# Strassen's scheme for the first layer's MLP, with the context's tokens as plain products on the same weight blocks

## The chip, the core and the metric

The kernel runs on one core of a Trainium2 chip. The metric is the device time of one execution in microseconds; the median over several executions is compared. Five engines work side by side, each through a list of instructions of its own: PE (TensorE, matrix products), DVE (VectorE), ACT (ScalarE), POOL (GpSimd) and SP (SyncE), which here only issues transfers. An instruction waits at the head of its engine's list until what it needs is there.

## What is computed

A network of two layers on 1024 latent tokens (`x`) and 256 context tokens (`ctx`), all in float32, with a model width of 1024. Layer 0 mixes tokens by attention, layer 1 by a state-space scan with a gated product behind it (GLU). After each mixer comes an MLP with a squared ReLU and 4096 hidden columns. Every norm is scaled and shifted, every residual gated, by vectors computed from conditioning weights `w_ada`. The context needs no MLP in layer 1.

```
def _mlp(h, w1, w2):
    return jnp.square(jax.nn.relu(h @ w1)) @ w2
...
    for i in range(DEPTH):
        need_ctx = i < DEPTH - 1
        m = act_lat @ w_ada[i] + b_ada[i]
        mc = act_ctx @ w_ada[i] + b_ada[i]
...
        x = x + g1 * y
        h2 = _rmsnorm(x, norm2_g[i], NORM_EPS) * (1.0 + sc2) + sh2
        x = x + g2 * _mlp(h2, mlp_w1[i], mlp_w2[i])
        if need_ctx:
            ctx = ctx + g1c * yc
            h2c = _rmsnorm(ctx, norm2_g[i], NORM_EPS) * (1.0 + sc2c) + sh2c
            ctx = ctx + g2c * _mlp(h2c, mlp_w1[i], mlp_w2[i])
    return _rmsnorm(x, final_g, NORM_EPS)
```

## The kernel before

Activations lie transposed: features on the 128 partitions, tokens along the free axis. The tokens are three blocks `BLK` (line 24): latent 0 and 1 of 512 each and the context, block 2, of 256. A float32 product is made of three fp32r matmuls, `hi*hi + hi*lo + lo*hi` (`mm3`, L328), so each operand is split first: ACT rounds the high part, DVE subtracts to get the low one (L324 and L325 for weight pages, L471 and L472 for tokens).

The stages in order are in_proj and attention, `out_proj` (L1118, matmuls into `op_acc`), the first layer's `mlp` (L1142, `m_acc`), the state-space stage (`ssm`, its first matmul is `s_X`, L1706), GLU, and the second layer's MLP `mlp_s` (L1187, `st_b`).

`out_proj` goes over the context's block first, then blocks 0 and 1. Column tile by column tile it adds the gated product to the residual streams `xl` and `xc` (L1109), which `load_x` fetches just before. `follow` with `rstd_steps` squares each finished column (L367), sums it over the partitions (L352) and so makes each token's norm factor: a power on POOL (L441), a Newton step on DVE (L447 to L449), and for a whole block a broadcast over the partitions in PSUM (`n_bc`, L398). `scaled` (L451) then multiplies the columns by it on DVE (`n_t`, L463, a ring of four tiles) and scales and shifts them on POOL (L465); `to_H` splits the result into `Hh` and `Hl`. Blocks 2 and 0 are done while `out_proj` goes on with the next block, block 1 while `mlp` has begun.

`mlp` goes over 16 slices `f` of 256 hidden columns: two weight pages for the first product, two for the second, three token blocks, 3 x 8 matmuls for each hidden tile and 3 x 2 for each output tile. Between its parts it calls `work`, a generator that does two things for later stages: 48 pages of conditioning weights of layer 1 (`ada`, L262: each page is a 512 KB load on SP's queue and eight small matmuls, L285), and 32 tables of powers for the state-space stage on POOL (`ssm_table`, L1556; its complex products are L1382 to L1387). With the last slice `last()` sets up `u_norm` (L1576), which makes the state-space stage's norm factors (`rU`, L1607) as columns are finished, copies the columns to DRAM (`xS`), and loads the gains `gU`.

`mlp_s` does the latent tokens of layer 1 by Strassen's scheme. There are four quarters of the hidden columns, and for each two units, one per weight matrix. In a unit, weights and tokens are 2 x 2 blocks, and seven products take the place of eight; each product is four k-tiles of 12 matmuls with 512 columns, so 8 x 336 = 2688 matmuls. Blocks of weights lie in a ring of five buffers `A`. Sums of weight blocks are made without an engine's arithmetic: `s1` is a load and a DMA on POOL's queue that adds a second block to it (`acc`, L1234); `s2` is `s1` negated by ACT (`neg`, L1239) with another block added; `s3` and `s4` likewise. ACT and DVE split each block (`st_a`, L1292 and L1295) and each token tile (`st_b`, L1304 and L1307); sums of token blocks are DVE's (L1219). The order on every engine is set by a planner, class `Plan` (L115): each step has an engine, a cost, a rank (due time) and steps that it needs, and the planner writes the engines' lists from these.

```
    ORDER = (1, 2, 6, 5, 7, 3, 4)
    AFTER = {6: 1, 7: 6, 4: 7, 5: 2, 3: 5}
```

## Time and profile before

| | |
|---|---|
| median of 3 runs | 3076.78 us (3076.42 to 3079.14) |
| profiled execution | 3081.73 us, span 3080.0 us |
| PE busy | 2878.7 us, 93% of the span |
| DVE, ACT, POOL busy | 1920.8, 1185.0, 1160.0 us |
| out_proj | 941.0 to 1060.5 us from the span's start |
| first layer's MLP | 1060.5 to 2003 us |
| ssm, then GLU | 2003 to 2222, to 2411 us |
| second layer's MLP | 2411 to 3080 us |

Times in the profile count from the start of the span. A group of instructions is listed with its source line, engine, operation, output and inputs, shape and count; behind the bar stand its busy time, the mean duration of one in ns, and how long its engine was idle just before such an instruction, with what ended the wait. Matmuls are pipelined: the duration of one overlaps the next, so the pace is read from start times. PEclk is the clock that TensorE was granted, 1.00 being 2.4 GHz.

### The profile page before, as it was taken

How to read it: one execution, taken by the hardware profiler on the slowest of the kernel's cores; microseconds unless marked ns; L12 is line 12 of the kernel's file. 1: busy time of each engine (PE TensorE's matmuls, PEld its weight loads, DVE VectorE, ACT ScalarE, POOL GpSimd, SP SyncE). 2: the span in 40 equal slices, each digit the busy share in tenths (PEclk: the TensorE clock that was granted, in tenths of full speed). 3: DMA queues.
4: the chain of work that ended last, by engine and by line, in shares of the span. 5: the costliest groups of instructions: out<-in, count | busy, mean ns of one | idle time of the engine just before them, and what ended most of it. 6: DMA issues, size and time to landing. Idle time of an engine off the chain costs nothing. (4 is left out here: it accounts for less than half of the span.)

```text
span 3080.0 us, 46255 instructions
## 1 busy us (share of the span) xinstructions
PE 2878.7 (93%) x17352; PEld 2377.3 (77%) x17352; DVE 1920.8 (62%) x3337; ACT 1185.0 (38%) x2211; POOL 1160.0 (38%) x2346
## 2 busy tenths in 40 slices
PE   7999998888999999999999999967699799999997
PEld 4878887777878777787888888856588688888885
DVE  3887686988664555554554545489923566666665
ACT  3322214676663321111112121245422365656563
POOL 3343233555442277777787000167623200000001
PEclk9999999999999999999999999988899899999998
DMA  6356664233543124333311111366432444554441
GB/s 241 110 187 220 206 221 143 70 90 104 154 118 140 55 97 128 108 120 101 76 60 48 44 41 42 101 184 182 125 108 75 111 117 126 125 126 125 125 110 55
DMA packets 172305, 363.47 MB, mean 118 GB/s; under 512 B 34689, under 2 KB 97185, under 8 KB 162865
## 3 DMA queue, kind: packets, MB, share of 16 engines
q1 hardware_dynamic: 162384, 310.62, 31.5%
q0 software_dynamic: 9696, 49.90, 7.5%
q8 instruction: 136, 2.23, 0.3%
q14 instruction: 89, 0.72, 0.1%
HBM read 294.97 MB, written 65.49 MB: 117 GB/s over the span
## 5 line engine op out<-in xcount | busy, mean ns | idle before, releaser
L1316 PE MATMUL st_b<-st_b,st_a 128*128 128x512 f32 x2688 | 614.2, 391 | 10.3 <-DVE st_b L1307 7.2
L1316 PEld LDWEIGHTS st_b<-st_b,st_a 128*128 128x128 f32 x2688 | 506.7, 189 | 117.8 <-DVE st_b L1307 7.8
L324 ACT ACTIVATE w_hi<-w_raw 128x1024 fp32r<-128x1024 f32 x132 | 136.7, 1053 | 460.6 <-PE m_acc L334 351.7
L333 PE MATMUL m_acc<-hid_h,w_hi 128*128 128x512 f32 (+1 forms) x768 | 277.1, 361 | 0.0
L333 PE MATMUL m_acc<-Hh,w_hi 128*128 128x512 f32 (+1 forms) x768 | 273.9, 357 | 0.0
L334 PE MATMUL m_acc<-hid_l,w_hi 128*128 128x512 f32 (+1 forms) x768 | 272.6, 355 | 0.0
L335 PE MATMUL m_acc<-Hh,w_lo 128*128 128x512 f32 (+1 forms) x768 | 272.3, 354 | 0.0
L335 PE MATMUL m_acc<-hid_h,w_lo 128*128 128x512 f32 (+1 forms) x768 | 272.1, 354 | 0.0
L334 PE MATMUL m_acc<-Hl,w_hi 128*128 128x512 f32 (+1 forms) x768 | 272.1, 354 | 0.0
L325 DVE TENSOR_TENSOR w_lo<-w_raw,w_hi 128x1024 fp32r<-128x1024 f32 x132 | 169.3, 1294 | 155.7 <-ACT w_hi L324 148.2
L1109 DVE SCALAR_TENSOR_TENSOR xl<-m_acc,m,xl 128x512 f32<-128x512 f32 x256 | 189.5, 747 | 116.4 <-PE m_acc L335 116.1
L1160 DVE TENSOR_TENSOR m_r<-m_r 128x512 f32<-128x512 f32 (+1 forms) x96 | 60.8, 635 | 229.0 <-ACT hid_h L1159 228.8
L333 PEld LDWEIGHTS m_acc<-hid_h,w_hi 128*128 128x128 f32 x768 | 145.0, 189 | 36.0 <-issue 14.4
L333 PEld LDWEIGHTS m_acc<-Hh,w_hi 128*128 128x128 f32 x768 | 145.7, 190 | 24.4 <-issue 4.5
L334 PEld LDWEIGHTS m_acc<-hid_l,w_hi 128*128 128x128 f32 x768 | 145.1, 189 | 22.9 <-issue 3.4
L335 PEld LDWEIGHTS m_acc<-Hh,w_lo 128*128 128x128 f32 x768 | 145.7, 190 | 20.3
L335 PEld LDWEIGHTS m_acc<-hid_h,w_lo 128*128 128x128 f32 x768 | 145.1, 189 | 20.6
L334 PEld LDWEIGHTS m_acc<-Hl,w_hi 128*128 128x128 f32 x768 | 145.7, 190 | 19.2
L1158 ACT ACTIVATE m_r<-m_acc 128x512 f32<-128x512 f32 (+1 forms) x96 | 50.1, 524 | 254.9 <-PE m_acc L335 254.0
L333 PE MATMUL ip_acc<-Hh,w_hi 128*128 128x512 f32 (+1 forms) x384 | 143.1, 374 | 4.1 <-ACT Hh L471 4.1
L334 PE MATMUL ip_acc<-Hl,w_hi 128*128 128x512 f32 (+1 forms) x384 | 139.3, 363 | 1.5 <-DVE Hl L472 1.2
L335 PE MATMUL ip_acc<-Hh,w_lo 128*128 128x512 f32 (+1 forms) x384 | 138.6, 362 | 0.0
(399 smaller groups left out, 6753.7 us busy)
## 6 DMA issues: line engine op xcount, KB each, us to landing
ada_raw<-in_wada_dram SPq DMA_DIRECT2D x96, 512.0 KB, 4.2
w_raw<-in_w_dram SPq DMA_DIRECT2D x64, 512.0 KB, 4.2
s_par<-pD SPq DMA_DIRECT2D x32, 864.0 KB, 4.5
at_q<-qD SPq DMA_DIRECT2D x152, 128.0 KB, 2.7
w_raw<-in_win_dram SPq DMA_DIRECT2D x24, 512.0 KB, 4.6
pD<-tb_cs POOLq DMA_DIRECT2D x32, 320.0 KB, 2.5
pD<-sl_w SPq DMA_DIRECT2D x16, 576.0 KB, 3.4
st_wa<-in_w1b_dram SPq DMA_DIRECT2D x9, 1024.0 KB, 6.3
```

The source lines that it names most:

```text
L324: nc.scalar.activation(hi[:, j], r, AF.Copy)
L325: nc.vector.tensor_tensor(lo[:, j], r, hi[:, j].bitcast(F32), ALU.subtract)
L333: nc.tensor.matmul(out, lh, rh, start=first and i == 0, stop=False)
L334: nc.tensor.matmul(out, lh, rl, start=False, stop=False)
L335: nc.tensor.matmul(out, ll, rh, start=False, stop=last and i == n - 1)
L1109: nc.vector.scalar_tensor_tensor(xv, av, gate, xv, op0=ALU.mult, op1=ALU.add)
L1158: nc.scalar.activation(r[:, :n], acc[:, :n], AF.Relu)
L1160: nc.vector.tensor_tensor(r[:, :n], r[:, :n], r[:, :n], ALU.mult)
L1316: PE.matmul(bk[p][:, mt], x, y, start=(p in (1, 2, 5) and t == 0 and i == 0), stop=(t == 3 and i == 2), skip_group_check=True)
```

## The change

Layer 0's MLP is now done by `mlp_s` too, called by `mlp0` for layer 0 and by `mlp1` for layer 1; `mlp` is gone. Each of layer 0's eight units has, beside its seven products, two plain ones for the context, `c1` ahead of them and `c2` behind them (`ctx_product`): eight k-tiles of 12 matmuls with 256 columns, on the blocks `w11`, `w12` and `w22`, `w21`. Per unit that makes 336 matmuls of 512 columns and 192 of 256. `w21` is one load more in a unit, and layer 0 has four buffers in ring `A`; layer 1 has six.

What `mlp` interleaved goes elsewhere. The 48 pages of conditioning weights move into `out_proj`, three steps of the generator after each column tile, with a ring of four pages. The gains `gU` are loaded there as well. The tables become 256 planner steps on POOL inside layer 0's `mlp_s` (`extra`). The norm factors of `out_proj`'s blocks are kept, and `norms()` scales all 24 columns behind `out_proj`, into float32 tiles `hr` that lie where `Hh` and `Hl` lay. In the last unit the squares for `u_norm` are planner steps after product 4 (both latent blocks) and after `c2` (context). In `mlp_s` of layer 0 the token sums share fewer tiles and are made again in each first unit; layer 1 keeps one of its three.

```diff
+    a["w1b"] = g["mlp_w1"].reshape(2, 2, 4, P, 4, 2, 512).transpose(0, 4, 5, 1, 3, 2, 6).reshape(2, 4, 2, 2, P, 2048)
+    a["w2b"] = g["mlp_w2"].reshape(2, 4, 2, 4, P, 2, 512).transpose(0, 1, 5, 2, 4, 3, 6).reshape(2, 4, 2, 2, P, 2048)
...
-    def out_proj(self, ps, sp):
+    def out_proj(self, ps, sp, prep):
...
         def then(b, bc):
-            self.scaled(lambda ct: self.xv0(ct, b), BLK[b][1], 0, 1, int(b == 2), bc, sp, self.to_H(b))
+            if b == 2:
+                rs[b] = sp.tile([P, BLK[b][1]], F32, name="n_bcc")
+                nc.scalar.activation(rs[b], bc, AF.Copy)
+            else:
+                rs[b] = bc
...
                     step(b, ct)
+                    prep()
...
         step()
-    def mlp(self, i, first, xv, ps, mp, prep, last):
...
+        def norms():
+            for b in (2, 0, 1):
+                scaled(b, rs[b], to=lambda ct: self.Hr[b][:, ct])
+        return norms
...
+        products = ("c1", *self.ORDER, "c2") if ctx else self.ORDER
+        for j, fn in enumerate(extra):
+            plan.add("G", 1.9, 4.0 + 2.9 * j, fn)
...
+                at[p] = now
+                now += 8 * 1.45 if p in ("c1", "c2") else 4 * PK
...
+            s1 = (u + ctx) % 2
+            X = {1: f"X{s1}", 2: f"X{1 - s1}", "c1": f"X{1 - s1}", "c2": f"X{1 - s1}"}
+            bk = {p: bank[s1 if p in (1, 6, 7, 4) else 1 - s1] for p in products}
...
+            if ctx:
+                ld["w21"] = D(at[1] + 40, F(load, "w21", (1, 0)), take=["A"])
...
+                if u == 7 and p in tail:
+                    x = [y for q in products[:products.index(p) + (p != lasts)] for t in range(4) for y in [made.get(("x", q, t))] if y]
+                    own = max(len(tail[p]) - 4, 0)
+                    for j, fn in enumerate(tail[p]):
+                        tailpe = plan.add("S", 0.6, e + 4 + 0.6 * j, fn, [*x, made["x", p, j - own] if p == lasts and j >= own else None, tailpe])
...
+    def ctx_product(self, p, u, plan, at, ld, hm, made, free, X, bk, A, T, sa, sb, hr, chid, xv, prev):
+        V, S, PE = self.nc.vector, self.nc.scalar, self.nc.tensor
+        second, m, n = u % 2, int(p == "c2"), NCTX
+        for j in range(8):
+            k = j if m == 0 else (j + 4) % 8
+            t, key, r = k % 4, f"w{m + 1}{k // 4 + 1}", at[p] + 1.45 * j
+            if t % 2 == 0:
+                sl = {}
+                def ahi(t=t, sl=sl, key=key):
+                    sl["a"] = T("a", sa)
+                    sl["w"] = A[key][:, t:t + 2]
+                    S.activation(sl["a"][:, 0], sl["w"], AF.Copy)
+                def alo(sl=sl):
+                    V.tensor_tensor(sl["a"][:, 1], sl["w"], sl["a"][:, 0].bitcast(F32), ALU.subtract)
+                ah = plan.add("S", 1.06, r - 9, ahi, [ld[key]], take=["a"])
+                al = plan.add("V", 1.24, r - 8, alo, [ah], give=[("A", ld[key])] if m else [])
+            x = (chid if second else hr[2])[:, k]
+            def bhi(t=t, sl=sl, x=x):
+                sl["b", t] = T("b", sb)
+                S.activation(sl["b", t][:, 0, :n], x, AF.Copy)
+            def blo(t=t, sl=sl, x=x):
+                V.tensor_tensor(sl["b", t][:, 1, :n], x, sl["b", t][:, 0, :n].bitcast(F32), ALU.subtract)
+            bh = plan.add("S", 0.41, r - 8, bhi, [hm["chid", k]] if second else [], take=["b"])
+            bl = plan.add("V", 0.41, r - 7, blo, [bh])
+            def mm(j=j, t=t, sl=sl):
+                l, h = sl["a"][:, :, t % 2], sl["b", t]
+                for mt in range(4):
+                    c = slice(P * mt, P * mt + P)
+                    for i, (x, y) in enumerate(((l[:, 0, c], h[:, 0, :n]), (l[:, 0, c], h[:, 1, :n]), (l[:, 1, c], h[:, 0, :n]))):
+                        PE.matmul(bk[p][:, mt, :n], x, y, start=(j == 0 and i == 0), stop=(j == 7 and i == 2), skip_group_check=True)
+            prev["pe"] = plan.add("PE", 1.45, r, mm, [al, bl, prev.get("pe")], take=[X[p]] if j == 0 else [], give=[("b", bh)] + ([("a", ah)] if t % 2 else []))
+            if j == 0:
+                made["X", p] = prev["pe"]
...
+    def tail(self, step):
+        return [F(step, 1, ct) for ct in (4, 5, 6, 7, 0, 1, 2, 3)] + [F(step, 0, ct) for ct in range(4)], [F(step, 0, ct) for ct in range(4, 8)]
...
+    def mlp1(self, mp, wp, ps):
...
+        blocks += [mp.tile([P, 4, 512], F32, name=f"st_wc{j}") for j in range(2)]
...
+        self.mlp_s(1, xv, self.Hr, blocks, sa, sb, hid, t2, tt, bank, {3: early, 4: late}, step)
...
+    def mlp0(self, mp, ps, rp):
+        blocks = [mp.tile([P, 4, 512], F32, name=f"st_w{j}") for j in range(4)]
...
+        sp, banks = self.shim([self.Hr[0][:, j] for j in range(4)], bank[0], u_lm=[tt[0][:, 0:P]])
+        step = self.u_norm(rp, sp, banks)
+        tables = self.ssm_tables(mp)
+        self.mlp_s(0, self.xv0, self.Hr, blocks, sa, sb, hid, None, tt, bank,
+                   {4: sum(self.tail(step), []), "c2": [F(step, 2, ct) for ct in range(KT)]}, step, chid, [F(next, tables)] * 256)
...
-        ends = {1: [0, 2, 4, 6, 7], 2: [0, 3, 7]}
+        ends = {0: [3, 5, 6, 7], 2: [0, 3, 7]}
...
+            rp = es.enter_context(net.pool("rms", side="right"))
+            net.bc_bufs = 2
+            with net.pool("ps2", 4, space=PSUM) as ps, tc.manual_schedule(engines={mybir.EngineType.Pool}):
+                with net.pool("ada", side="right") as ap, net.pool("nrm", side="right") as sp:
+                    ada = net.ada([(1, n) for n in range(12)], ps, ap, ap, 4)
+                    def prep():
+                        for _ in range(3):
+                            next(ada, None)
+                    norms = net.out_proj(ps, sp, prep)
+                    if stop("out_proj"):
+                        return
+                    for _ in ada:
+                        pass
+                    net.ada_gain(1, 0)
+                    net.ada_gain(1, 1)
+                    hs.close()
+                    hr = hs.enter_context(net.pool("hr0"))
+                    net.Hr = [hr.tile([P, KT, BLK[b][1]], F32, name=f"hr{b}") for b in range(3)]
+                    norms()
+            net.bc_bufs = 1
+            with net.pool("mlp0") as mp, net.pool("ps6", space=PSUM) as ps:
+                net.mlp0(mp, ps, rp)
```

How the built programs differ at three places. First SP, whose list is the order of its transfers, from the residual streams at the start of out_proj (`in_wout` are pages of out_proj's weights, `in_wada` of conditioning weights, 512 KB each). Before:

```order
L1093 DMA xl<-in_xs_dram 128x2x1024 x4
L1095 DMA xc<-in_cs_dram 128x8x256
L323 DMA w_raw<-in_wout_dram 128x1024 x2
L274 DMA ada_raw<-in_wada_dram 128x1024 x2
L323 DMA w_raw<-in_wout_dram 128x1024 x8
L323 DMA w_raw<-in_w_dram 128x1024 x6
```

In the change:

```order
L1091 DMA xl<-in_xs_dram 128x2x1024 x4
L1093 DMA xc<-in_cs_dram 128x8x256
L273 DMA ada_raw<-in_wada_dram 128x1024 x18
L322 DMA w_raw<-in_wout_dram 128x1024 x2
L273 DMA ada_raw<-in_wada_dram 128x1024 x4
L322 DMA w_raw<-in_wout_dram 128x1024 x2
```

Eighteen conditioning pages now stand between the residual streams and the next two pages of out_proj's weights, which before came right behind the streams.

Second DVE, from the last norm factors of out_proj's last latent block (`n_v`, `rs_t`, `n_r`). Before:

```order
L389 TENSOR_SCALAR n_v<-n_tk 128x4
L447 TENSOR_TENSOR rs_t<-rs_y 128x4
L448 SCALAR_TENSOR_TENSOR rs_t<-rs_t,n_v 128x4
L449 SCALAR_TENSOR_TENSOR n_r<-rs_t,rs_y 128x4
L463 TENSOR_TENSOR n_t<-xl,n_bc 128x512 x3
L472 TENSOR_TENSOR Hl_100<-n_t,Hh_97 128x512 x2
L463 TENSOR_TENSOR n_t<-xl,n_bc 128x512
L472 TENSOR_TENSOR Hl_100<-n_t,Hh_97 128x512
L463 TENSOR_TENSOR n_t<-xl,n_bc 128x512
L472 TENSOR_TENSOR Hl_100<-n_t,Hh_97 128x512
```

In the change, from the last residual adds of out_proj to the first splits of product `c1`:

```order
L1107 SCALAR_TENSOR_TENSOR xl<-op_acc,m_87,xl 128x8x64 x3
L388 TENSOR_SCALAR n_v<-n_tk 128x4
L446 TENSOR_TENSOR rs_t<-rs_y 128x4
L447 SCALAR_TENSOR_TENSOR rs_t<-rs_t,n_v 128x4
L462 TENSOR_TENSOR n_t<-xc,n_bcc 128x256
L448 SCALAR_TENSOR_TENSOR n_r<-rs_t,rs_y 128x4
L462 TENSOR_TENSOR n_t<-xc,n_bcc 128x256 x3
L462 TENSOR_TENSOR n_t<-xl,n_bc 128x512 x16
L1373 TENSOR_TENSOR st_a<-st_w_10753,st_a 128x1024
L1383 TENSOR_TENSOR st_b<-hr_10670,st_b 128x256 x2
L1373 TENSOR_TENSOR st_a<-st_w_10753,st_a 128x1024
L1383 TENSOR_TENSOR st_b<-hr_10670,st_b 128x256 x3
```

All remaining `n_t` columns now stand ahead of the first weight split, where before they alternated with the splits of the same block while matmuls of other blocks ran.

Third ACT at the end of the first MLP (`n_sq` squares, `n_e` sums copied out of PSUM, `rU` norm factors spread for the state-space stage). Before, the last block's part, between which matmuls still ran:

```order
L367 ACTIVATE n_sq<-xc 128x256 x5
L1607 ACTIVATE rU<-u_r 128x64
L367 ACTIVATE n_sq<-xc 128x256 x3
L382 ACTIVATE n_e<-n_st 128x256
L1693 ACTIVATE s_w_19127<-s_par_19118 64x4x144 x2
L1607 ACTIVATE rU<-u_r 128x32
```

In the change, from the last split of `c2` (`st_b<-st_hc`) on; the tiles of `hr` hold the squares:

```order
L1380 ACTIVATE st_b<-st_hc 128x256
L366 ACTIVATE hr_10668<-xl 128x512 x8
L381 ACTIVATE hr_10668<-st_b_10768 128x512
L366 ACTIVATE hr_10668<-xl 128x512
L1685 ACTIVATE rU<-st_b_10768 128x64
L366 ACTIVATE hr_10668<-xl 128x512 x7
L381 ACTIVATE hr_10668<-st_b_10768 128x512
L366 ACTIVATE hr_10668<-xc 128x256
L1685 ACTIVATE rU<-st_b_10768 128x64
L366 ACTIVATE hr_10668<-xc 128x256 x7
L381 ACTIVATE hr_10668<-st_b_10768 128x256
L1685 ACTIVATE rU<-st_b_10768 128x32
```

The squares of both latent blocks, which stood ahead of the last context columns, now stand behind the last split.

## Rows read from the trace of the kernel before

**Rows 1.** Busy by stage: window, length, PE, PEld, DVE, ACT, POOL, PEclk, DMA share, GB/s.
```profile
941.00:1060.50 119.50, 116.28 (x621) 98.32 (x622) 52.94 (x78) 36.03 (x57) 32.27 (x30) 1.00 0.32 115
1060.50:2003.00 942.50, 940.35 (x5142) 776.71 (x5144) 471.51 (x709) 190.06 (x304) 503.87 (x1685) 1.00 0.25 80
```

**Rows 2.** The same view, a stretch inside the second layer's MLP.
```profile
2506.00:2584.00 78.00, 78.00 (x346) 64.59 (x345) 61.28 (x85) 41.42 (x64) 3.47 (x4) 1.00 0.51 128
```

**Rows 3.** Timeline of PE, first MLP's start; start us, us, engine line op.
```profile
1061.84 0.28 PE L333 MATMUL m_acc<-Hh,w_hi 128*128 128x256 f32 x1
...
1062.80 0.28 PE L335 MATMUL m_acc<-Hh,w_lo 128*128 128x256 f32 x1
```

**Rows 4.** Costliest groups (x count | busy, mean ns | idle before, releaser), two of PE's.
```profile
L1316 PE MATMUL st_b<-st_b,st_a 128*128 128x512 f32 x2688 | 614.2, 391 | 10.3 <-DVE st_b L1307 7.2
...
L333 PE MATMUL m_acc<-Hh,w_hi 128*128 128x512 f32 (+1 forms) x768 | 273.9, 357 | 0.0
```

**Rows 5.** Timeline of PE at the first MLP's end.
```profile
2001.51 0.28 PE L335 MATMUL m_acc<-hid_h,w_lo 128*128 128x256 f32 x1
...
2010.87 1.49 PE L1706 MATMUL s_X<-s_U,s_par 128*64 128x160 f32 x7 [3.91 <-DMA s_par<-pD]
```

**Rows 6.** Timeline of PE around one load of conditioning weights.
```profile
1096.83 0.40 PE L335 MATMUL m_acc<-hid_h,w_lo 128*128 128x512 f32 x1
1097.16 0.64 PE L285 MATMUL ada_acc<-ada_raw,act 128*32 128x256 f32 x8
...
1098.07 0.40 PE L334 MATMUL m_acc<-hid_l,w_hi 128*128 128x512 f32 x1
```

**Rows 7.** Busy time in ten microseconds of out_proj (columns of rows 1).
```profile
951.00:961.00 10.00, 8.63 (x71) 8.34 (x70) 3.34 (x7) 3.37 (x7) 2.25 (x3) 1.00 1.04 410
```

**Rows 8.** Timeline of ACT and POOL at the second MLP's start.
```profile
2414.21 0.63 ACT L367 ACTIVATE n_sq<-xl 128x512 f32<-128x512 f32 x1 [2.23 <-POOL xl L1823]
...
2418.88 1.02 POOL L441 TENSOR_TENSOR rs_y<-n_v,mhalf 128x4 f32<-128x4 f32 x1 [4.71 <-DVE n_v L389]
```

**Rows 9.** Groups by form in out_proj, POOL's scalings.
```profile
L465 POOL TENSOR_SCALAR n_t<-n_t,G,m 128x512 f32<-128x512 f32 x8 | 7.7, 962 | 11.2 <-DVE n_t L463 11.0
...
L465 POOL TENSOR_SCALAR n_t<-n_t,G,m 128x256 f32<-128x256 f32 x8 | 6.4, 806 | 6.4 <-DVE n_t L463 6.2
```

**Rows 10.** Busy time at the second MLP's start (columns of rows 1).
```profile
2422.00:2430.00 8.00, 1.05 (x4) 0.54 (x3) 7.34 (x11) 0.00 (x0) 6.55 (x7) 0.50 0.00 0
2430.00:2440.00 10.00, 9.70 (x36) 7.90 (x37) 9.01 (x12) 2.22 (x3) 3.55 (x3) 0.82 0.78 188
```

**Rows 11.** Second MLP's start: DMA issues (us to landing) and ACT's negations by form.
```profile
st_wb<-in_w1b_dram POOLq DMA_DIRECT2D x3, 1024.0 KB, 8.1
st_wa<-in_w2b_dram SPq DMA_DIRECT2D x3, 1024.0 KB, 6.1
...
L1239 ACT ACTIVATE st_wa<-st_wa 128x512 f32<-128x512 f32 x20 | 11.3, 617 | 0.0
```

**Rows 12.** Groups by form over the span, DVE in the second MLP.
```profile
L1341 DVE SCALAR_TENSOR_TENSOR xl<-st_b,m,xl 128x512 f32<-128x512 f32 x112 | 78.6, 744 | 42.2 <-PE st_b L1316 42.2
...
L1307 DVE TENSOR_TENSOR st_b<-st_h,st_b 128x512 fp32r<-128x512 f32 x96 | 63.7, 684 | 11.1 <-ACT st_b L1304 11.1
...
L1295 DVE TENSOR_TENSOR st_a<-st_wa,st_a 128x1024 fp32r<-128x1024 f32 x46 | 56.2, 1221 | 36.5 <-ACT st_a L1292 36.5
```

**Rows 13.** Stretch with tables (busy, two DVE groups by form), then 1720 to 1980 without.
```profile
1100.00:1650.00 550.00, 549.91 (x3053) 446.44 (x3052) 275.99 (x411) 99.55 (x156) 430.00 (x1491) 1.00 0.31 97
...
L325 DVE TENSOR_TENSOR w_lo<-w_raw,w_hi 128x1024 fp32r<-128x1024 f32 x36 | 44.7, 1262 | 32.7 <-ACT w_hi L324 32.5
L1160 DVE TENSOR_TENSOR m_r<-m_r 128x512 f32<-128x512 f32 x37 | 28.1, 759 | 110.5 <-ACT hid_h L1159 110.3
...
L325 DVE TENSOR_TENSOR w_lo<-w_raw,w_hi 128x1024 fp32r<-128x1024 f32 x17 | 20.4, 1220 | 16.3 <-ACT w_hi L324 16.3
L1160 DVE TENSOR_TENSOR m_r<-m_r 128x512 f32<-128x512 f32 x20 | 13.8, 690 | 69.3 <-ACT hid_h L1159 69.3
```

More of the change, by code (lines that the diff above doesn't have):

```diff
@@ L1203, in mlp_s @@
+        rings = dict(A=[(f"A{j}",) for j in range(len(blocks))], a=[(f"a{j}",) for j in range(2)], b=[(f"b{j}",) for j in range(4)], X0=[("X0",)], X1=[("X1",)])
         plan = Plan(rings, lead=10.0)
@@ L1298, in mlp_s @@
                         ah = plan.add("S", 1.06, r - 9, ahi, [wa], take=["a"])
[L1299 removed]
+                        gv = [("A", ld[key])] if p != 6 and not (ctx and p == 4) else []
                         al = plan.add("V", 1.24, r - 8, alo, [ah], give=gv)
@@ L1325, in mlp_s @@
                 e, outs = at[p] + 4 * PK, []
-                free[p] = outs
-                for t in range(4):
-                    x11, x12, x21, x22 = (xv(m, n, t) for m in range(2) for n in range(2))
+                free.setdefault(p, outs)
+                for t in range(4) if p not in ("c1", "c2") else ():
+                    x11, x12, x21, x22 = (xv(4 * m + t, n) for m in range(2) for n in range(2))
                     c11, c12, c21, c22 = (hid[m, n][:, t] for m in range(2) for n in range(2))
@@ L1362, in mlp_s @@
                             outs.append(made["x", p, t])
-                if last and p in (3, 4):
-                    for m in (1, 0) if p == 3 else (0, 1):
-                        for t in range(4):
-                            tail = plan.add("S", 0.6, e + 4 + 0.6 * t, F(step, int(p == 3), 4 * m + t),
-                                            [*(made["x", q, i] for q in (2, 7, p) for i in range(4)), tail])
-            base += 28 * PK
+                if u == 7 and p in tail:
[3 more added lines that the diff above has]
+                        tailpe = plan.add("S", 0.6, e + 4 + 0.6 * j, fn, [*x, made["x", p, j - own] if p == lasts and j >= own else None, tailpe])
+            for t in range(4):
+                prev[4, t] = halves[4, t, "b"]
+            base = now
         ET = mybir.EngineType
@@ L1374, in mlp_s, with xa @@
                 s["fn"]()
-            step()
-        self.plan = plan
+            last()
+    def ctx_product(self, p, u, plan, at, ld, hm, made, free, X, bk, A, T, sa, sb, hr, chid, xv, prev):
[31 more added lines that the diff above has]
+                made["X", p] = prev["pe"]
+        for t in range(4):
+            ct, rk = 4 * m + t, at[p] + 11.6 + 0.1 * t
+            ps = bk[p][:, t, :n]
+            if second:
+                def xa(x, ps=ps, ct=ct):
+                    V.scalar_tensor_tensor(x, ps.rearrange("p (s c) -> p s c", s=8), self.mv(0, 5, ct, 1), x, op0=ALU.mult, op1=ALU.add)
+                made["x", p, t] = plan.add("V", 0.49, rk, F(xa, xv(ct, 2)), [prev["pe"]], give=[(X[p], made["X", p])])
+            else:
+                x = plan.add("S", 0.4, rk, F(S.activation, chid[:, ct], ps, AF.Relu), [prev["pe"]], give=[(X[p], made["X", p])])
+                hm["chid", ct] = plan.add("S", 0.41, rk + 0.5, F(S.activation, chid[:, ct], chid[:, ct], AF.Square), [x])
```

236 lines of the change are left out of this document (98 added, 138 removed).

## The prediction

> **What bounds the kernel now.** I read the busy time by stage first. In the first layer's MLP, 1060.5 to 2003 us, PE is busy 940.4 of 942.5 us at a granted clock of 1.00 [rows 1], so what it saves in matmuls is time, as long as what feeds PE keeps up. The second question is what one matmul costs. The other MLP is the model: in one of its stretches PE issues 346 matmuls of 512 columns in 78.0 us, 0.2254 us each, and is never idle [rows 2]. In the timeline of the first MLP eight matmuls of 256 columns start 0.96 us apart, 0.12 us each [rows 3]. The mean durations of the grouped rows (0.36 to 0.39 us) overlap and are no price. Third, counts: six groups of 768 m_acc matmuls, of which a third has 256 columns [rows 4], so 3072 and 1536; Strassen's MLP has 2688 st_b [rows 4].
>
> The profiled execution took 3081.7 us, 5.0 above the median of the three runs, 3076.8; the sum is made against the first, and the difference is carried over. A difference under 0.2% (6 us) can't be told from none here.
>
> **The change part by part.** I add up one stretch, from out_proj's first matmul (941.7) to the first matmul of the state-space stage, s_X at 2010.9 [rows 5]: 1069.2 us before. Up to its start the instruction order is the same on every engine. Behind it, second MLP included, I take no change: its two buffers more and its sums computed again in each unit move work beside a PE that waits 10.3 us in all there [rows 4]; plus or minus 2 us.
>
> *Out_proj.* Before it takes 119.5 us [rows 1], 118.8 from its first matmul. It now holds all 48 loads of the conditioning weights of layer 1. One load is eight matmuls: in the timeline m_acc starts at 1096.83, the load follows, and the second m_acc after it starts at 1098.07 [rows 6]; 1.24 less two matmuls of 0.2254 is 0.79 us. 48 x 0.79 = 37.9 us, which leave the MLP, so they are moved, not added; the transposes after them go along, 3 us (an estimate). New is a wait: SP now issues 18 of these pages (0.5 MB each) between the 5 MB of residual streams and weight pages 7 and 8 of out_proj, so 15 MiB lie ahead of the last two column tiles of the context's block. At 410 GB/s, which the DMA engines reach at 951 to 961 [rows 7], that takes until about 982, with the split 985. PE has 144 context matmuls (17 us) and 18 loads (14 us) until then, so is ready at 973: 12 us of waiting. It is 0 if the residual streams are waited for anyway, 20 if pages are held back. The small transfers for the gains go through SP's queue here too; I cost them at nothing, as pages are fetched a ring of four ahead, and at a few us, inside the bound, if that cover is gone. Sum: 118.8 + 38 + 3 + 12 = 172 us (160 to 182); out_proj's last matmul ends near 1113.
>
> *Before the MLP's first matmul.* This is zero now, as the norms of two blocks are scaled during out_proj. In the change all 24 columns are scaled behind it, since their tiles lie where H lay. The start of the second MLP shows the chain: the last square begins at 2414.21 and the power on POOL at 2418.88, 4.7 us later; it takes 1.0 [rows 8]. With the residual add ahead, POOL starts scaling 6.6 us after out_proj. On DVE all n_t stand ahead of the first split. Their ring has 4 tiles, so the last waits for the 20th scaling: 8 x 0.81 + 12 x 0.96 = 18.0 us [rows 9]. Then n_t, one weight split (1.22) [rows 12] and a context split (about 0.4): 26.9, say 27 us (20 if POOL is started earlier by the free context columns, 32 with some contention).
>
> *The MLP.* 2688 x 0.2254 + 1536 x 0.12 = 606 + 184 = 790 us. The same prices give 692 + 184 = 877 for the old order; the other 66 of its 942.5 are the 48 loads (38), their transposes, the norms' matmuls and small waits, all of which go elsewhere or away. So the saving in the matmuls themselves is 384 x 0.2254 = 87 us. To 790 I add a slow start. In the second MLP PE's granted clock was 0.50 (1.2 GHz) in the 8 us in which it waited for the norm, and 0.82 in the next 10 [rows 10]; the first sum of weight blocks now stands on POOL behind the 24 scalings and the first table pieces, takes 8.1 us to land and four negations of 0.62 [rows 11], and product 6 waits for it. I take 12 us for both (4 to 25), and 4 us for scattered waits: 806.
>
> *Does the feeding keep up?* DVE: a second-layer unit holds 22 weight splits of 1.22, 28 token splits and 16 sums of 0.68, 28 residual adds of 0.74 [rows 12] and 24 instructions of half the width for the context (at 0.45, an estimate between half and all of the price of 512 columns): 89 us in the 98.7 us that PE needs for a unit (336 x 0.2254 + 192 x 0.12). The second MLP's such units hold, by the same prices and counts of 14, 28, 16 and 28, 68 of 76 us, and PE doesn't wait there [rows 2]. New is that POOL runs the state-space tables beside it. POOL is busy 430 of 550 us while the tables run in the old MLP [rows 13]; there the DVE square of 512 columns takes 759 ns, after them 690; the weight split 1262, then 1220 [rows 13]. So 10% on the short and 3% on the long ones, about 5 us a unit: 94 of 98.7. It fits, narrowly. By the Trainium skill, "SBUF — State Buffer", section "Who interferes with whom", a DVE instruction with two SBUF inputs and a GpSimd instruction that reads SBUF exclude each other for a whole instruction. The rows agree in direction only: they show a tenth, not a doubling. POOL itself had some 620 us of tables and now also 32 accumulating DMAs; it has 790.
>
> *The tail.* Before, the norm of the last context columns is all that is left: last matmul 2001.51, s_X 2010.87, 9.4 us [rows 5]. In the change ACT's order puts the squares of both latent blocks behind the last context split, then three norm chains one after the other: 24 squares (16 of 0.63 [rows 8], 8 at 0.4, 13.3 us), three chains through the power of some 6 us each as there, and 3 us for the first states, about 35 us from a start some 4 us ahead of the last matmul: 31, say 32 (20 if the chains overlap, 40 if not).
>
> Sum: 172 + 27 + 806 + 32 = 1037 against 1069.2: 32 us less. Profiled 3050, by the median **3045 us**. So PE stands for 78 us in four new places (pages 12, norms 27, start and scatter 16, tail 23 more than before), against 87 us of matmuls and 25 us of norms and small waits of the old MLP that fall away (66 less the 41 that move).
>
> **The rivals.**
> (A) *The stands are shorter*: no wait for pages (0), 20 us of norms, 6 at the start, a tail of 22. The stretch is then 160 + 20 + 796 + 22 = 998, 71 less: 3006. For it: the chains were added up as if nothing overlapped. Against: the orders of DVE and ACT are fixed, and PE has nothing else to do in them.
> (B) *The sums of the weight blocks come late in each unit; this ends on the other side.* With four block buffers instead of five, block s2 is made from s1 by a load (6 us), an accumulating DMA on POOL's queue (8.1), four negations (2.5) and a second accumulating DMA (8.1) [rows 11], some 32 us with the splits after the buffer is free, and product 6 wants it about 10 us later than that. POOL is busy with tables, so each accumulate can wait for pieces queued ahead. Once the chain is more than 10 us late PE waits in each of eight units; from 4 us each on (32 in all) the gain is gone, at 10 us each the time is 3045 + 80 = 3125. Against: a table piece lasts 1.9 us in the plan, and the second MLP, with the same lead, waits nowhere in steady state [rows 2].
> (C) *DVE becomes the bound in second-layer units while tables run.* A table instruction lasts 430/1491 = 0.29 us, and one is running 78% of the time [rows 13]. If each of the 82 splits and sums of a unit waits for a whole one, that adds 18 to 89: 107 or 108 us in place of 98.7, so some 9 us in each of three or four units under tables, 26 to 35 us: 3071 to 3080, no change. Against: the measured tenth. The Trainium skill's rule named above is the one by which this would happen.
> That the change doesn't do what it says is excluded by the counts in the built order (2688 and 1536 matmuls).
>
> **How the numbers follow.** My forecast, 0.60: all four bounds at once would give 3006 or 3089, which I don't expect, so 3020 to 3070; (A) 0.20, 3000 to 3020; (C) 0.10, 3065 to 3085; (B) 0.10, 3070 to 3130. The range 3002 to 3074 takes in the forecast, (A) and half of (C), and leaves out little more than (B). Faster by over 6 us: forecast and (A) and half of (C), 0.84; the same: 0.07; slower, (B) and a little of (C): 0.09.
>
> **What would show it.** In the changed profile: st_b x2688 with 512 and x1536 with 256 columns; a PE wait of about 12 us in out_proj ended by a weight page or its split; about 27 us without matmuls behind out_proj at a lower granted clock after; an MLP of about 806 us with DVE over 90% in second units; about 32 us from the last MLP matmul to s_X, ended by ACT and the norm chain. Waits of PE at product 6 on a split of s2 in every unit would show (B); waits on DVE splits in second units alone, (C).

## The result, and the profile after the change

The change makes the kernel slower: 3154.36 us median (3153.14 to 3155.91, four runs) against 3076.60, a ratio of 1.0251 with a 95% interval of 1.0233 to 1.0269. I had forecast 3045, in a range of 3002 to 3074.

| | before | after |
|---|---|---|
| profiled span | 3080.0 us | 3153.7 us |
| PE busy | 2878.7 us (93%) | 2815.0 us (89%) |
| DVE, ACT, POOL busy | 1920.8, 1185.0, 1160.0 us | 2097.9, 1499.5, 1340.2 us |
| out_proj's first matmul to s_X | 1069.2 us | 1146.1 us |

The counts are as announced. These are PE's two groups of the page (count | busy, mean ns | idle before, releaser); L1294 holds both layers and L1392 the context's products:

```profile
L1294 PE MATMUL st_b<-st_b,st_a 128*128 128x512 f32 x5376 | 1235.8, 392 | 50.3 <-ACT st_a L1270 37.0
...
L1392 PE MATMUL st_b<-st_b,st_a 128*128 128x256 f32 x1536 | 195.9, 290 | 54.6 <-ACT st_b L1380 39.2
```

So 384 matmuls are gone, and 105 us of idle time stand in these two groups, where Strassen's MLP had 10.3 before [rows 4]. PE's waits over the whole kernel name what ended them (total us, times, longest):

```profile
PE st_b L1392 <- ACT st_b L1380: 39.2, 4, 11.6
PE st_b L1294 <- ACT st_a L1270: 37.0, 3, 15.2
...
PE s_X L1784 <- DMA s_par<-pD: 19.0, 2, 18.0
...
PE st_b L1392 <- DVE st_b L1383: 15.4, 1, 15.4
```

The first two are new and lie inside the first layer's MLP, the third is in the tail and the fourth at the MLP's start. In PE's timeline the four stretches of the forecast can be measured; out_proj begins at 939.9 here, the rows are out_proj's last matmul, the MLP's first steady one, two of its waits, its last group and s_X:

```profile
1118.82 0.39 PE L334 MATMUL op_acc<-Hh,w_lo 128*128 128x512 f32 x1
...
1143.78 6.43 PE L1392 MATMUL st_b<-st_b,st_a 128*128 128x256 f32 x35 [15.39 <-DVE st_b L1383]
...
1382.09 8.14 PE L1294 MATMUL st_b<-st_b,st_a 128*128 128x512 f32 x23 [15.16 <-ACT st_a L1270]
...
1494.46 3.17 PE L1392 MATMUL st_b<-st_b,st_a 128*128 128x256 f32 x12 [11.58 <-ACT st_b L1380]
...
2037.06 1.69 PE L1392 MATMUL st_b<-st_b,st_a 128*128 128x256 f32 x12
...
2085.96 4.48 PE L1784 MATMUL s_X<-s_U,s_par 128*64 128x160 f32 x37 [18.00 <-DMA s_par<-pD]
```

| stretch | forecast | after |
|---|---|---|
| out_proj, to 1119.2 | 172 | 179.3 |
| norms, to 1143.8 | 27 | 24.6 |
| MLP, to 2038.8 | 806 | 895 |
| tail, to 2086.0 | 32 | 47.2 |
| sum | 1037 | 1146.1 |

Behind s_X the rest takes 1067.7 us, before 1069.1: no change there, as assumed. The miss is the MLP's 89 us, the tail's 15 and 7 in out_proj, less 2 in the norms.

In the MLP seven waits of 6.9 to 15.2 us add up to 76.2, one in each unit from the second on: at the last k-tile of `c1` in the second-layer units, at product 1 in the first-layer ones. Of the 105 us over its 790 some 29 are left, and 17 of them are the clock behind each wait. In windows of the busy view (length, PE, PEld, DVE, ACT, POOL, PEclk, DMA share, GB/s) the 7 us behind the wait that ends at 1494.46 show a mean granted clock of 0.61, which is some 5 us at 0.50 (1.2 GHz) and the rest at 1.00; a later window without a wait shows 1.00 throughout:

```profile
1494.46:1501.46 7.00, 6.75 (x24) 5.50 (x25) 6.04 (x10) 5.49 (x9) 3.56 (x8) 0.61 0.28 43
1515.00:1540.00 25.00, 25.00 (x112) 20.68 (x111) 21.11 (x29) 10.50 (x15) 15.11 (x43) 1.00 0.69 171
1150.00:1945.00 795.00, 717.28 (x3746) 617.97 (x3745) 537.14 (x724) 447.01 (x762) 666.49 (x1669) 0.95 0.40 108
```

In the 7 us behind each of the seven waits the granted clock is 0.55 to 0.76 in the mean; 7 us times what is missing to 1.00, added up, is the 17 us. Another 10 the MLP takes over its 790 even without such waits (experiment 3). The last row holds nearly the whole MLP: POOL is busy 84% of it, more than ACT or DVE. What a wait is made of stands in the timeline of all engines before the third unit:

```profile
1346.51 0.33 SPq L1205 DMA_DIRECT2D st_w<-in_w1b_dram  x1
...
1372.01 0.91 POOL L1208 DMA_DIRECT2D st_w<-in_w1b_dram  x1 [0.28 <-issue]
...
1379.94 1.15 ACT L1213 ACTIVATE st_w<-st_w 128x512 f32<-128x512 f32 x2 [16.66 <-DMA st_w<-in_w1b_dram]
1381.00 1.04 ACT L1270 ACTIVATE st_a<-st_w 128x1024 fp32r<-128x1024 f32 x1
...
1382.09 2.48 PE L1294 MATMUL st_b<-st_b,st_a 128*128 128x512 f32 x4 [15.16 <-ACT st_a L1270]
...
1383.38 0.89 POOL L1208 DMA_DIRECT2D st_w<-in_w1b_dram  x1 [7.65 <-ACT st_w L1213]
```

The first block of sum `s1` is fetched from 1346.5 on, and a 1 MB load lands after some 5 us. The DMA that adds the second block is issued on POOL 25 us after the fetch, and by its row it waits for nothing but its turn (0.28 us of issue). When it lands, ACT, which has stood at the head of its list with a negation for 16.7 us, goes on; the split of product 1's weights stands behind that negation, and PE starts again one instruction later. So PE's next product needs no sum at all; it is held by a negation ahead of it in ACT's list, the negation by the accumulate, and the accumulate by the table pieces ahead of it in POOL's list. All seven waits look so: ACT stands at the first negation of `s2` for 8.7 to 16.7 us, and in the second-layer units it is the last context split of `c1` that stands behind it.

The pieces themselves got longer. Two of the six groups of the tables' products on POOL, after the change:

```profile
L1457 POOL TENSOR_TENSOR tb_cs<-tb_cs,tb_t 128x64 f32<-128x64 f32 (+6 forms) x256 | 121.1, 473 | 20.1
...
L1453 POOL TENSOR_TENSOR tb_t<-tb_ep,tb_cs 128x64 f32<-128x64 f32 (+6 forms) x256 | 105.9, 414 | 0.0
```

The same two before:

```profile
L1387 POOL TENSOR_TENSOR tb_cs<-tb_cs,tb_t 128x64 f32<-128x64 f32 (+6 forms) x256 | 86.6, 338 | 20.0
...
L1383 POOL TENSOR_TENSOR tb_t<-tb_ep,tb_cs 128x64 f32<-128x64 f32 (+6 forms) x256 | 73.0, 285 | 0.0
```

All six together take 658.8 us; before they took 485.3. In the planner's list a piece costs 1.9 us, which is 485.3/256. It now takes 2.57, with the table's transfers and memsets 2.75. The same trace shows what makes them longer. Two pieces of equal size on POOL, the second of which begins just behind a weight split of DVE:

```profile
1345.22 0.20 POOL L1455 TENSOR_TENSOR tb_cs<-tb_ep,tb_cs 128x2 f32<-128x2 f32 x1
1345.27 1.22 DVE L1373 TENSOR_TENSOR st_a<-st_w,st_a 128x1024 fp32r<-128x1024 f32 x1
1345.37 1.18 POOL L1456 TENSOR_TENSOR tb_t<-tb_ep,tb_cs 128x2 f32<-128x2 f32 x1
```

Of the 1536 table products 605 overlap no DVE instruction and last 260 ns in the mean; 225 overlap only DVE instructions that read one of their two inputs from PSUM (L1316, L1319 and L1401) and last 255; 706 overlap one with both inputs in SBUF (splits and sums) and last 629. In the kernel before the three means are 257, 261 and 583, but only 271 products meet the third kind.

### The profile page after: what moved, and what is told of

Read it like the earlier page. It is cut to its first block, busy times and chain, and to the rows that moved or that the text cites. A ratio compares the mean times of both kernels' runs of the same rounds, so it can differ in the third digit from the quotient of the medians.

```text
span 3153.7 us, 46679 instructions
## 1 busy us (share of the span) xinstructions
PE 2815.0 (89%) x16968; PEld 2327.8 (74%) x16968; DVE 2097.9 (67%) x3533; ACT 1499.5 (48%) x2764; POOL 1340.2 (42%) x2377
## 5 line engine op out<-in xcount | busy, mean ns | idle before, releaser
L1294 PE MATMUL st_b<-st_b,st_a 128*128 128x512 f32 x5376 | 1235.8, 392 | 50.3 <-ACT st_a L1270 37.0
L1294 PEld LDWEIGHTS st_b<-st_b,st_a 128*128 128x128 f32 x5376 | 1016.1, 189 | 268.2 <-ACT st_a L1270 37.6
L1392 PE MATMUL st_b<-st_b,st_a 128*128 128x256 f32 x1536 | 195.9, 290 | 54.6 <-ACT st_b L1380 39.2
L1392 PEld LDWEIGHTS st_b<-st_b,st_a 128*128 128x128 f32 x1536 | 193.1, 198 | 58.1 <-ACT st_b L1380 40.1
L1273 DVE TENSOR_TENSOR st_a<-st_w,st_a 128x1024 fp32r<-128x1024 f32 x112 | 140.5, 1255 | 110.0 <-ACT st_a L1270 109.6
L1319 DVE SCALAR_TENSOR_TENSOR xl<-st_b,m,xl 128x512 f32<-128x512 f32 x224 | 157.7, 743 | 54.0 <-PE st_b L1294 53.9
L1282 ACT ACTIVATE st_b<-st_h 128x512 fp32r<-128x512 f32 x208 | 128.8, 623 | 98.4 <-PE st_b L1294 88.1
L1285 DVE TENSOR_TENSOR st_b<-st_h,st_b 128x512 fp32r<-128x512 f32 x208 | 142.7, 703 | 24.8 <-ACT st_b L1282 23.7
L748 PE MATMUL at_sc<-at_k,at_q 128*128 128x256 f32 (+2 forms) x608 | 125.4, 337 | 8.8 <-ACT at_p L838 4.9
L1457 POOL TENSOR_TENSOR tb_cs<-tb_cs,tb_t 128x64 f32<-128x64 f32 (+6 forms) x256 | 121.1, 473 | 20.1
L1824 PE MATMUL s_y<-s_w,s_s 128*128 128x256 f32 x256 | 80.8, 468 | 49.8 <-DVE s_s L1816 47.2
L1322 ACT ACTIVATE st_h<-st_h 128x512 f32<-128x512 f32 x224 | 120.6, 620 | 0.0
L1454 POOL TENSOR_TENSOR tb_cs<-tb_cs,tb_t 128x64 f32<-128x64 f32 (+6 forms) x256 | 106.9, 418 | 20.1
```

The costliest lines, as they stand in the source:

```text
L748: PE.matmul(sc[:, c:c + n], qd["q"][:, m, hl, qo:qo + P], k["k"][m][:, k0:k0 + n], start=(hl == 0), stop=(hl == 1))
L1273: V.tensor_tensor(sl["a"][:, 1], sl["w"], sl["a"][:, 0].bitcast(F32), ALU.subtract)
L1282: S.activation(sl["b", t][:, 0], x, AF.Copy)
L1285: V.tensor_tensor(sl["b", t][:, 1], x, sl["b", t][:, 0].bitcast(F32), ALU.subtract)
L1294: PE.matmul(bk[p][:, mt], x, y, start=(p in (1, 2, 5) and t == 0 and i == 0), stop=(t == 3 and i == 2), skip_group_check=True)
L1319: V.scalar_tensor_tensor(x, bk[p][:, t].rearrange("p (s c) -> p s c", s=x.shape[1]), g, x, op0=ALU.mult, op1=ALU.add)
```

## The experiments

Three theories. **P**: POOL's list holds more work than the MLP lasts, so the accumulates come late. **B**: four block buffers are too few, so the loads come late. **N**: only the place of the negations in ACT's list is wrong.

**1. The planner's cost of a table piece.**

```diff
-            plan.add("G", 1.9, 4.0 + 2.9 * j, fn)
+            plan.add("G", 2.75, 4.0 + 2.9 * j, fn)
```

> One number: the planner's cost of a table piece, 1.9 to 2.75 us, so about 33 instead of 37 pieces stand on POOL between the same accumulating DMAs of two units. Theory P (POOL holds more work than the MLP lasts, so the accumulates stand 15 to 20 us behind table pieces, ACT waits at the head of its list for s1's sum, and PE waits 9 to 15 us in each unit): PE's waits at the unit changes (77 us in the changed kernel) fall under 25 us, the first MLP takes 810 to 835 us instead of 895, the time is 3070 to 3100. Theory B (four block buffers, the loads come too late): the buffers are as before, so the waits stay, 3140 to 3160. Theory N (only the place of the negations on ACT): the same as B, 3140 to 3160.

Measured: 3174.33 us, ratio 1.0304 (1.0288 to 1.0319), the MLP 910 us. No theory said that. Its trace, in the unit that starts near 1600:

```profile
1592.27 0.90 POOL L1208 DMA_DIRECT2D st_w<-in_w1b_dram  x1 [6.91 <-DVE st_b L1383]
...
1621.33 4.28 ACT L1213 ACTIVATE st_w<-st_w 128x512 f32<-128x512 f32 x8
...
1623.83 0.92 POOL L1208 DMA_DIRECT2D st_w<-in_w1b_dram  x1 [20.59 <-ACT st_w L1213]
...
1635.72 4.62 PE L1294 MATMUL st_b<-st_b,st_a 128*128 128x512 f32 x9 [7.24 <-ACT st_a L1270]
```

The accumulate of `s1` is now on time (its load was issued at 1586.3), and lands near 1600. But the negations, which wait for nothing, stand 20 us later in ACT's list, the accumulate of `s2` waits for them, and PE waits at product 6 instead of product 1. The plan books an accumulate as 8 us of POOL; with 33 pieces of 2.75 us (34 or 35 stand in a steady unit of the trace) its POOL is fuller than a unit lasts, so it expects the sum late and puts the negations late. P in its simple form falls: the place of the accumulates isn't all.

**2. The negations of s2 due 22 us later.**

```diff
-                ng.append(plan.add("S", 0.6, at[1] - 10 + t, F(neg, "s2", "s1", t),
+                ng.append(plan.add("S", 0.6, at[1] + 12 + t, F(neg, "s2", "s1", t),
```

> The four negations of s2 are due 22 us later in ACT's list (behind the splits of product 1), POOL's list nearly the same. Theory N (head of ACT's list): product 1 no longer waits, 3090 to 3110. Theory P: POOL still has some 100 us of table pieces and sums per unit ahead of the sums, so the wait moves from product 1 to product 6 and the time stays within 20 us of the changed kernel, 3135 to 3155. Theory B: as P.

Measured: 3179.64 us in one run, the MLP 920. N falls: product 1 no longer waits, and the wait comes back at product 6 (6.9 to 17.0 us in the first seven units), as P had it, though the time is 25 us over P's bound. This run does not part P from B, for which the same was expected. One of the waits in PE's timeline:

```profile
1429.42 0.79 PE L1294 MATMUL st_b<-st_b,st_a 128*128 128x512 f32 x1 [17.01 <-ACT st_a L1270]
```

**3. The tables out of the MLP.** The first attempt took the steps out of the plan and left the pieces to the scheduler behind it:

```diff
-        ..., step, chid, [F(next, tables)] * 256)
+        ..., step, chid)
+        for _ in tables:
+            pass
```

> All 256 table pieces stand behind the first MLP instead of inside it; the order of the other engines is the planner's own. The whole gets longer by the tables' own time, which now nothing hides (485 to 620 us), so only the MLP's stretch counts. Theory P: the MLP takes 795 to 815 us, no accumulate waits longer than 2 us behind its block's landing. Theory B: waits of 9 to 15 us per unit stay, 880 us or more. The tables' own pieces, with DVE idle, show what they take undisturbed: 1.9 us each if DVE slows them in the MLP, 2.7 us if they are simply that long.

Measured: 3384.69 us, and it told nothing of B: the scheduler put the pieces into POOL's list ahead of accumulates, and PE waited 107 and 109 us at two of them. The second attempt issues them in the hand-made order, behind the last norm.

> As the run before meant it: the 256 table pieces stand last in POOL's list of the first MLP, behind the last norm, and the plan of the other engines holds no tables. The whole is longer by the tables (485 to 650 us) and says nothing; the MLP's stretch counts. Theory P (tables on POOL's list hold up the sums): the MLP takes 795 to 820 us from its first steady matmul to its last, against 895; PE waits over 1.5 us sum to under 10 us. Theory B (four block buffers): waits of 9 us and more in each unit stay, 870 us or more. Contention (DVE and POOL slow each other): a table piece takes 1.9 to 2.1 us with DVE idle, against 2.7.

Measured: 3493.27 us for the whole, as expected of tables that nothing hides. The MLP takes 800 us, from 1147.5 to 1947.5, and PE waits nowhere in it for more than 1 us. Its busy view (columns as above):

```profile
1150.00:1550.00 400.00, 399.33 (x2121) 346.21 (x2120) 293.53 (x418) 247.36 (x417) 13.98 (x16) 1.00 0.41 106
1550.00:1940.00 390.00, 389.34 (x2044) 336.21 (x2044) 284.63 (x405) 241.50 (x407) 13.14 (x15) 1.00 0.38 99
```

B's reason falls: with the same four buffers every load and sum is on time. And 800 is 6 us under the forecast's 806, 790 of matmuls and 16 for start and scatter. The tables now take 405 us, with DVE busy for 7 of the 452 us in which they run; the same two groups:

```profile
L1459 POOL TENSOR_TENSOR tb_cs<-tb_cs,tb_t 128x64 f32<-128x64 f32 (+6 forms) x256 | 69.8, 273 | 20.1
...
L1455 POOL TENSOR_TENSOR tb_t<-tb_ep,tb_cs 128x64 f32<-128x64 f32 (+6 forms) x256 | 65.9, 257 | 0.0
```

So a piece is 1.58 us with DVE nearly idle (I had put down 1.9 to 2.1), 1.90 beside the old MLP, 2.57 beside the new one. DVE hardly suffers. Its weight and token splits from 1250 to 1940, after the change:

```profile
L1273 DVE TENSOR_TENSOR st_a<-st_w,st_a 128x1024 fp32r<-128x1024 f32 x84 | 105.8, 1260 | 92.3 <-ACT st_a L1270 91.9
...
L1285 DVE TENSOR_TENSOR st_b<-st_h,st_b 128x512 fp32r<-128x512 f32 x84 | 60.1, 730 | 11.7 <-ACT st_b L1282 11.6
```

and without tables beside it:

```profile
L1273 DVE TENSOR_TENSOR st_a<-st_w,st_a 128x1024 fp32r<-128x1024 f32 x98 | 119.8, 1223 | 60.9 <-ACT st_a L1270 60.6
...
L1285 DVE TENSOR_TENSOR st_b<-st_h,st_b 128x512 fp32r<-128x512 f32 x108 | 72.5, 687 | 15.4 <-ACT st_b L1282 15.1
```

The short splits of the context's input tokens suffer more, 529 ns against 420.

**4. True prices in the plan.** A piece of 2.75 us, and an accumulate as 0.9 us of POOL (its row above) and 8 us more until it lands, by a step on an engine `Q` that exists only in the plan:

```diff
-GD = lambda rank, fn, after=(), give=(): plan.add("G", 8.0, rank, fn, after, give=give)
+GD = lambda rank, fn, after=(), give=(): plan.add("Q", 8.0, rank, F(int), [plan.add("G", 0.9, rank, fn, after)], give=give)
```

> The planner is given what the trace shows: a table piece 2.75 us, an accumulating DMA 0.9 us on POOL and 8 us more until it lands, where the plan had 1.9 us and 8 us on POOL. No work is changed, only the order. Theory P: the accumulates stand where their blocks land, the MLP takes 810 to 850 us, the time is 3075 to 3115. If the planner's greedy order is no better with true prices, since POOL is full (36 pieces of 2.75 us in a unit of 98.7), 3130 to 3160.

> As the run before with 3.0 us for a table piece, so that 32 pieces fall on each unit and POOL has some 10 us of slack in a unit. Theory P: 3060 to 3095, with PE waits in the MLP under 20 us in all. Theory B: no less than 3130.

> Only the accumulating DMA is priced as the trace shows it (0.9 us on POOL, 8 us more to land), the table piece stays at 1.9 us. Without the 8 us in which the plan kept POOL from tables, 48 pieces stand on POOL in a unit instead of 37. Theory P: POOL's list sets the unit: 48 x 2.7 + 4 x 0.9 = 133 us for five units, then 99: an MLP of some 970 us in place of 895, 3200 to 3240. If wrong landing times in the plan were the fault and not POOL's load, 3080 to 3120.

The first two were run together, the third later.

| piece in the plan | accumulate in the plan | time, us | MLP, us |
|---|---|---|---|
| 1.9 | 8 on POOL (the change) | 3154 | 895 |
| 2.75 | 8 on POOL | 3174 | 910 |
| 1.9 | 0.9 on POOL, 8 to land | 3178 | 918 |
| 2.75 | 0.9, 8 to land | 3114 | 852 |
| 3.0 | 0.9, 8 to land | 3086 | 824 |

No work differs between these five, only the order; the last three rows are single runs. 3114 and 3086 lie in the ranges that P gave them, 3178 in neither of the two ranges given. With the true landing alone 39 to 47 pieces fall on a steady unit, and the busy view shows POOL at 92% and PE waiting while tables last, then PE at full pace without them:

```profile
1250.00:1350.00 100.00, 76.06 (x381) 64.78 (x380) 64.23 (x87) 39.71 (x66) 91.73 (x255) 0.88 0.40 107
1950.00:2050.00 100.00, 99.67 (x530) 86.25 (x530) 77.27 (x111) 53.94 (x89) 3.44 (x4) 1.00 0.34 84
```

That is P's mechanism (PE waits 13 to 24 us at each change of unit while tables last), but less of it than P had put down, 3200 to 3240. With 3.0 us, 33 to 35 pieces fall on a steady unit, about as many as in experiment 1, and it is some 88 us faster, since ACT's list now fits too. In the fifth unit the negations of `s2` start 9 us behind the issue of `s1`'s accumulate; in the unit shown for experiment 1 it was 29. Two windows:

```profile
1250.00:1350.00 100.00, 99.57 (x531) 86.19 (x531) 83.20 (x116) 50.37 (x79) 92.70 (x226) 1.00 0.44 120
1550.00:1650.00 100.00, 95.22 (x477) 80.40 (x477) 64.96 (x86) 68.05 (x118) 92.74 (x236) 0.98 0.45 123
```

The second row has two short waits (1.5 and 3.1 us); the first four units have none over 1 us. What holds is a wider P: the lists of POOL and ACT must both fit when a sum really lands, and it went better with fewer pieces in a unit (35 or 36 with 852 us, 33 to 35 with 824). In P's first wording one thing is wrong: in total POOL has room. 256 pieces of 2.75 us and 32 accumulates of 0.9 make 733 us, and the MLP without tables lasts 800. But in the changed kernel 35 to 37 pieces stand between the sums of one steady unit and the next, and the last of all ends at 1941.8, 97 us ahead of the MLP's end: with four accumulates a unit's list is 100 to 105 us, where PE needs 98.7.

**5. The tail.** After the change the loads of the state-space stage are issued right behind the last norm factor:

```profile
2068.01 0.20 ACT L1685 ACTIVATE rU<-st_b 128x32 f32<-128x32 f32 x1 [3.64 <-PE st_b L1684]
2068.04 0.33 SPq L1763 DMA_DIRECT2D s_par<-pD  x1
...
2074.41 6.65 SPq L1736 DMA_DIRECT2D s_U<-xS  x8
```

The small operand `u_lm` lies in a raw weight page (`tt`), and with the weight pools moved to the bottom of memory the stage's parameter tiles reuse it.

```diff
-        sp, banks = self.shim(..., u_lm=[tt[0][:, 0:P]])
+        sp, banks = self.shim(..., u_lm=[chid[:, 4, 0:P]])
```

> The last norm's small operand u_lm lies in the context's hidden tile instead of the raw weight page, over which the state-space stage's first parameters lie. If that reuse holds their load back (it is issued at 2068.0, right behind the last read of u_lm, and s_X starts at 2086.0), the loads go 25 us earlier, s_X starts 10 to 17 us earlier, 3137 to 3145. If the transfers of the last context columns to DRAM and back hold s_X anyway, less than 5 us.

Measured: 3143.68 us, ratio 1.0200 (1.0181 to 1.0218). The loads of `s_T` and `s_par` start at 2041.3, the MLP's end, and s_X at 2076.0, 34.7 us behind the MLP instead of 47.2:

```profile
2041.34 3.64 SPq L1752 DMA_DIRECT2D s_T<-KD  x8
2045.03 0.90 SPq L1763 DMA_DIRECT2D s_par<-pD  x2
2060.22 3.14 POOL L1696 DMA_DIRECT2D xS<-xc  x2
2066.46 4.03 SPq L1736 DMA_DIRECT2D s_U<-xS  x8
```

What is left is the norm chain and the context columns' way to DRAM: POOL issues their last copies at 2060.2, `s_U`, which reads them, is fetched from 2066.5 on, and its landing ends PE's last wait.

**6. The pages in out_proj.** One generator step per column tile in the context's block, four in the latent ones, in place of three:

```diff
-                        for _ in range(3):
+                        for _ in range(1 if b == 2 else 4):
```

> The changed kernel with nothing but the order of the conditioning pages in out_proj (one step per column tile in the context's block, four in the latent ones). If the 18 pages ahead of the weight pages make out_proj's wait, out_proj's last matmul comes 8 to 14 us earlier, 3138 to 3148; if the residual streams make it, less than 4 us, 3150 to 3156.

Measured: 3149.33 us in one run. Out_proj's last matmul starts at 1108.3 instead of 1118.8, but its first at 933.8 instead of 939.9, ahead of anything that the edit touches. Out_proj itself, from first matmul to last, takes 174.5 us against 178.9: 4.4 us less, where kernels with the old order spread from 177.2 to 181.1. So the order of the pages is worth some 4 us (8 between the two kernels of experiment 7), between the two things expected (8 to 14, or under 4). PE's waits in the changed kernel's out_proj show why: little of it was a wait for weight pages.

```profile
PE ada_tp L300 <- DVE ada_e L293: 9.7, 7, 2.5
PE op_acc L332 <- DVE xc L1107: 4.1, 1, 4.1
PE ada_acc L284 <- DMA ada_raw<-in_wada_dram: 2.7, 3, 1.8
PE op_acc L332 <- ACT w_hi L323: 1.0, 1, 1.0
```

PE waited for the transposes of the conditioning rows (`ada_tp`), for a residual add and for the pages themselves, and came to the weights of the seventh column tile so late (990.1, forecast 973) that it waited 1.5 us for their two parts.

**7. Together.** Spread tables and tail; then also the pages, and every second column behind out_proj scaled by ACT:

```diff
+            if half and ct % 2:
+                nc.scalar.activation(o, t[:, :n], AF.Identity, bias=self.mv(i, part, ct, m), scale=G[:, ct, m:m + 1])
+            else:
                 nc.gpsimd.tensor_scalar(o, t[:, :n], ...)
```

> The spread tables (3.0 us a piece in the plan, accumulates 0.9 on POOL and 8 to land) and u_lm in the context's hidden tile together. The two mend different stretches, so by theory P their gains add: 69 us of the first and 11 of the second off the changed kernel's 3154, 3070 to 3080, that is no change against the kernel before. If the tail's loads only wait for something else once the MLP is faster, 3082 to 3090.

> As the run before, and out_proj fetches conditioning pages one step per column tile in the context's block and four in the latent ones (instead of three), and every second column of the norms behind out_proj is scaled on ACT instead of POOL. Out_proj loses its wait of some 12 us and the gap ahead of the first MLP falls from 26 to about 20: 12 to 20 us less than the run before, 3052 to 3065, which would be faster than the kernel before. If out_proj's pages come late because the queue is full anyway, only the 5 us of the norms: 3068 to 3075.

Measured: the first 3068.23 us, ratio to the kernel before 0.9958 (0.9941 to 0.9974); the second 3051.70 us (3048.8 to 3055.0), ratio 0.9905 (0.9888 to 0.9922). Both are faster than the kernel before, by 0.4% and 1.0%, and neither interval reaches 1; the first is 2 us and the second 0.3 us below the range that I had put down. The busy view of the second in out_proj and in the MLP:

```profile
934.60:1105.30 170.70, 155.50 (x1049) 113.45 (x1048) 57.16 (x86) 33.19 (x53) 17.34 (x14) 0.97 0.69 223
...
1124.00:1944.00 820.00, 805.40 (x4227) 691.74 (x4228) 616.54 (x832) 496.77 (x838) 703.34 (x1692) 0.99 0.42 114
```

Its out_proj begins at 934.6 and ends at 1105.3, the MLP runs from 1124.4 to 1944.8, s_X begins at 1978.3: 171, 19, 820 and 34 us, 1044 in all, against 1069 before. That this is near the forecast's 1037 says nothing for the forecast, which was for the kernel without these edits.

## Why the prediction was wrong

- **The matmuls** were right: 384 fewer, and 800 us for the MLP where nothing disturbs it.
- **The step that failed** is the last sentence of "Does the feeding keep up?": "POOL itself had some 620 us of tables and now also 32 accumulating DMAs; it has 790." It asked only whether POOL's load fits in the whole stretch, and by the whole stretch it does fit, 733 us at the measured prices. The 620 looks like no load: over 618 us (1082.8 to 1700.7) the tables run in the kernel before, 84 us of waiting for transfers included; the pieces with their transfers held POOL for 530. The runs show a load that grows (405, 485 or 659 us for the same instructions, by what DVE does beside it) and a list in which the place counts: 35 to 37 pieces in a unit, 100 to 105 us with the accumulates, where PE needs 98.7. So the term that failed is "4 us for scattered waits": seven waits of 76 us, and 17 us of lower clock behind them. I had read the contention in [rows 13] on DVE alone, where it is a few per cent, and not looked at POOL's own rows for it. Of the rule of the Trainium skill that I cited ("SBUF — State Buffer", "Who interferes with whom") this case shows the other side: weight splits grew from 1223 to 1260 ns and token splits from 687 to 730 on DVE, but POOL's pieces from 257 to 414 and from 273 to 473 in the groups shown. The kind of DVE instruction agrees with the rule (255 ns beside one SBUF input, 629 beside two). That every piece waits for the whole instruction is not shown: 1.18 against 0.20 us in the rows above looks so, but others that begin inside a split end before it.
- **Rival B** came true in its main point, accumulates that wait for pieces queued ahead, and nearly at its price: 10 us a unit, 3125, was the example; seven waits of 11 us on average and the clock behind them were measured, and 3154 lies above its 3130 too. I gave it 0.10. Two reasons against it were bad. "A table piece lasts 1.9 us in the plan" was the price beside the old MLP's work, and the second MLP, which waits nowhere, has no tables beside it. It was also placed one step off: PE waited at product 1 and `c1`, not product 6, since ACT's list let the negation hold up splits that needed no sum. And the four buffers, which B blamed as well, had no part in it.
- **Rival C** did not happen: DVE had work for 68% of the MLP (537 of 795 us in the window above) and was not what ended PE's waits there.
- **Norms** 24.6 for 27: the mechanism as described. **Out_proj** 179.3 for 172: near in size, but with luck. Of the 12 us put down to weight pages behind conditioning pages 1.5 were there; waits of 16.5 us for transposes, a residual add and the pages themselves stood in their place, and experiment 6 gave back 4.4.
- **The tail** was mis-sized: 47.2 for 32. The norm chains took 29 us to the last `rU`, as reckoned; what I missed is that the first loads behind them share memory with the last norm's operand, so they were added instead of hidden. Experiment 5 took 12.5 us of it away.
- **A slip in the sum**: the upper bounds of the four terms, 182, 32, 819 and 40, give 3081 and not 3089. Nothing else was worked out from it.

That DVE's work is the reason why POOL's pieces are longer rests on three points (DVE nearly idle, before, after) and on the overlaps counted inside each trace: the 706 products that meet a DVE instruction with two SBUF inputs account for 260 us over the mean of the others, and the tables lasted 254 us longer than beside an idle DVE. No run changed DVE's work alone beside the same tables.

## What to carry to other kernels

An order written from a cost table is only as good as its costs, and an in-order engine passes a wrong one on: a late sum on POOL held ACT, and ACT held a PE that lacked nothing. Before moving work beside other work, price it by rows taken under the load it will meet, check that it fits between two deadlines and not only in the whole stretch, and give the planner a transfer's issue and its landing as two things. When pools are laid out anew, ask what the next stage's first loads now lie on.
